# Retention's swish and row scales through Exp and Ln on ScalarE, PSUM banks from one free list, norm by tile at the start, final norm scaled ahead

## Chip, cores and metric

One Trainium2 chip, all 8 cores (two dies: cores 0 to 3 and 4 to 7). Each core computes one of the 8 batch elements; the cores exchange nothing. The metric is the time of the slowest core in microseconds (us) on the device.

Executions fall into two states: both kernels showed both, and so did 16 of the 18 kernels of the experiments. In the fast state all cores show nearly the same granted TensorE clock (0.977 to 0.982 of full speed in every fast execution of the kernel before). In the slow state the cores of one die, or of both, show a lower granted clock (0.81 to 0.98 in the runs of this study; in one execution of c15, 5663.94 us, 0.831 to 0.835 on one die and 0.993 to 0.994 on the other) and the time is up to 20% longer. This document compares fast executions alone.

Terms used below: PE is TensorE's matmul, DVE is VectorE, ACT is ScalarE, POOL is GpSimd, SP is the engine that issues most loads and stores other than weights. A *stage* is the time from the first matmul of one kind to the first matmul of the next kind.

## The reference, cut to what matters

```python
h   = modulate(rmsnorm(x, norm1_g), sh1, sc1)       # sh1, sc1, gt1...: silu(c) @ w_mod + b_mod
p   = h @ w_in                                      # q, k, v, g, u, vs, two merge gates
ret = bidirectional_retention(rope(q), rope(k), v, ...)             # 8 heads, starts from context
ret = ret * rsqrt(mean(ret * ret, -1) + EPS) * silu(g)              # row scale, swish
sg  = gelu(u) * (w_s @ layernorm(gelu(vs)) + b_s)                   # spatial mixing, 128x128
x   = x + gt1 * ((sig(gr) * (ret @ w_ret_o) + sig(gs) * (sg @ w_sg_o)) @ w_out)
h2  = modulate(rmsnorm(x, norm2_g), sh2, sc2)
x   = x + gt2 * ((silu(h2 @ w_a) * (h2 @ w_b)) @ w_ffn_out)
out = rmsnorm(x, final_norm_g)
```

Per core: 2048 positions, width 2048, 256 context positions, FFN width 5632. After the heads everything runs in two halves of 1024 positions.

## The kernel before

Program order is issue order on each engine (what that costs shows in the changed kernel's trace below, where x lands from 41.8 us on and ACT starts to norm it at 156.9); the writer of the kernel decides it by hand. SBUF tiles come from one pool of addresses, so a tile that is requested may have to wait until an earlier tile at that address is free. Weights stream through four 1 MB slots, requested by POOL.

The start. Conditions (`stA`), four x tiles and small tables are loaded; the first x tiles are normed; the decay tables are built and stored; then 16 modulation weights are used, each with its own small addition on DVE.

```python
for i, src in enumerate((c_in, cctx, n1g, n2g, lng, lnb)):
    tk = F.dma("sp", stA[16 * i:16 * (i + 1), :], src)
F.wait("pool", tk)              # no weight is requested before these landed
WS.pump()
...
load_x(xkeys[:4])
F.dma("sp", dist[:], distd); F.dma("sp", idx[:], idxd); F.dma("sp", jdx[:], jdxd)
F.dma("sp", wsf[:], sgw.rearrange("g i j -> i g j"))
...
norm_x(0, xkeys[0:4])           # ACT squares four tiles, DVE root, DVE scales four tiles
...                             # decay tables: DVE, ACT Exp, stores to tab_d
for s in range(16):
    mod_cols(s, bank(s % 4))    # 32 matmuls, then DVE adds b_mod into modp
```

The root (reciprocal square root) is 13 small DVE operations, used in every norm:

```python
def rsqrt(dst, src, n, mul):
    ... 4 operations, then three Newton steps of 3 operations on [128, n]
```

A retention head, its output block, with PSUM banks taken in turn from two fixed sets (`RA` of four, `RV` of two):

```python
def outp(b):
    ps = bank(RA.get())
    ...                                                     # 12 matmuls
    for i in range(2):
        F.act(r[:, i, :], ps[...], AF.Square, accum=ssq[:, i:i + 1])
    rsqrt(rst[:], ssq[:], 2, 1.0 / 256.0)                   # 13 DVE operations
    for i in range(2):                                      # only now is the bank read out
        F.stt("dve", r[:, i, :], ps[...], rst[:, i:i + 1], sg[:, i, :], ALU.mult, ALU.mult)

def g_unit(b, wg):
    ps = tm_pair(wg, ...)                                   # bank from RV
    F.act(sg, ps, AF.Silu)
```

Ahead of the spatial mixing the retention results, a bias table and row sums; ahead of the residual the x tiles and gate rows; at the end the final norm, all on DVE:

```python
F.dma("sp", part, ret_d[...])  # 16 loads
F.dma("sp", bsb, sgb.partition_broadcast(128))
...                            # row sums of w_s by two matmuls
rsqrt(rst[:], ssq[:], 1, 1.0 / D)
for q in range(4):
    F.stt("dve", xs, xs, rst[:], fngb[:, q * 512:(q + 1) * 512], ALU.mult, ALU.mult)
```

## Time and profile before

| | before |
|---|---|
| fast executions | 5043.67, 5044.09 us |
| profiled execution, slowest core | 5041.4 us |
| PE busy | 4655.7 us, 92% |
| matmuls at their closest spacing (estimate) | 4598 us |

The estimate counts every matmul of the trace at the spacing seen in undisturbed stretches: 216 ns for 512 columns, 109 ns for 256, 56 ns for 128, 25 ns for the two-column ones. Some 443 us are thus not matmul time, and only they can be won.

The page of the kernel before, part 1 (busy time, share of the span, number of instructions):

```profile
span 5041.4 us, 68033 instructions; the slowest of 8 cores (5014.0 to 5041.4 us)
PE 4655.7 (92%) x26671; PEld 2460.9 (49%) x26671; DVE 1438.4 (29%) x3076; ACT 803.0 (16%) x1577; POOL 483.3 (10%) x556
```

What PE waited for in the kernel before, whole span (us in total, how often, longest):

```profile
PE ps L279 <- DMA wm<-w_mod: 64.4, 10, 11.2
PE ps L279 <- DVE modp L303: 55.0, 1, 55.0
...
PE ps L279 <- DVE sTt L303: 26.5, 16, 2.2
PE ps L282 <- DVE wsb L312: 26.2, 1, 26.2
PE ps L279 <- DVE tm L307: 21.3, 7, 14.8
PE ps L279 <- DVE r L307: 21.2, 8, 3.0
...
PE ps L282 <- DVE xb L300: 18.1, 4, 15.4
```

Read: one single wait of 55 us for the addition into `modp` at the start; about 45 us in the heads (`sTt`, `r`), in pieces of 1.2 to 3.0 us; single waits in head 0 (`wsb`, `xb`) and in the mixing (`tm`).

### The profile page before, as it was taken

Reading aid. Unit: us, or ns where it says so; the run is one execution under the profiler, and the core shown is the slowest. Engines: PE = TensorE matmul, PEld = TensorE weight load, DVE = VectorE, ACT = ScalarE, POOL = GpSimd, SP = SyncE. Lnnn points to the kernel's source line nnn. Section 1 sums busy time; section 2 is a strip of 40 time slices with the busy share of each in tenths; the row PEclk is TensorE's granted clock in tenths of the full one; section 3 lists DMA queues with packets and bytes.
Section 4 is the critical chain, followed back from the end, with each engine's and each line's share of the span. In section 5 each row is a group of like instructions: output and inputs, shape, how many; then the busy total and the mean of one; then the engine's idle time right before and its main releaser. Section 6 shows DMA issues by size and latency. Waiting matters only on the chain.

```text
span 5041.4 us, 68033 instructions; the slowest of 8 cores (5014.0 to 5041.4 us)
## 1 busy us (share of the span) xinstructions
PE 4655.7 (92%) x26671; PEld 2460.9 (49%) x26671; DVE 1438.4 (29%) x3076; ACT 803.0 (16%) x1577; POOL 483.3 (10%) x556
## 2 busy tenths in 40 slices
PE   0479999999999899999999999899999999999996
PEld 0357667676664444444444444344444444444443
DVE  1244554444553311114112111434101230021015
ACT  2232222222222100013000000121000130000001
POOL 0012222122220011100000000000111000000000
PEclk9889999999999999999999999999999999999998
DMA  7743343332444434463444445554354634444443
GB/s 164 182 113 60 60 80 62 73 58 53 76 74 75 93 68 90 85 130 69 78 78 81 78 80 116 117 113 84 67 96 78 136 67 79 83 79 78 78 87 95
DMA packets 106729, 443.13 MB, mean 88 GB/s; under 512 B 10832, under 2 KB 36784, under 8 KB 63920
## 3 DMA queue, kind: packets, MB, share of 16 engines
q0 software_dynamic: 47232, 339.76, 38.2%
q1 hardware_dynamic: 59184, 99.04, 6.4%
q8 instruction: 216, 3.54, 0.3%
q14 instruction: 97, 0.79, 0.1%
HBM read 744.93 MB, written 33.57 MB: 154 GB/s over the span
## 4 chain that ended last, share of the span: by engine, by line
PE 82%; DVE 7%; DMA 5%; issue 3%; ACT 2%; SPq 1%; DVEq 0%; another core or an unknown queue 0%; ACTq 0%; POOL 0%; POOLq 0%
PE ps L279 81%; DMA xt<-x 1%; DVE rs_t L303 1%; PE ps L282 1%; SPq L260 1%; DVE rs_m L300 1%; DMA wm<-w_mod 1%; DMA x_35252<-x 1%; DVE rst L307 1%; DMA x_22924<-x 0%; DMA wk<-w_qkvg 0%; ACT r L293 0%; ACT xb L293 0%; DVE xb L300 0%; DVEq L182 0%
## 5 line engine op out<-in xcount | busy, mean ns | idle before, releaser
L279 PE MATMUL ps<-h,wfi 128*128 128x512 bf16 x5632 | 1221.5, 379 | 0.0
L279 PEld LDWEIGHTS ps<-h,wfi 128*128 128x128 bf16 x5632 | 549.9, 98 | 657.1
L279 PE MATMUL ps<-wfo,aT 128*128 128x512 bf16 x2816 | 608.4, 379 | 0.0
L279 PEld LDWEIGHTS ps<-wfo,aT 128*128 128x128 bf16 x2816 | 275.5, 98 | 332.3
L303 DVE TENSOR_TENSOR aT<-sa,ps 128x512 bf16<-128x512 f32 x176 | 121.0, 688 | 1065.0 <-PE ps L279 1057.3
L293 ACT ACTIVATE sa<-ps 128x512 f32<-128x512 f32 x176 | 104.9, 597 | 1370.9 <-PE ps L279 1370.9
L303 DVE TENSOR_TENSOR gtf<-ps,gtf 128x512 f32<-128x512 f32 x128 | 88.6, 692 | 778.7 <-PE ps L279 778.7
L279 PE MATMUL ps<-wv,h 128*128 128x256 bf16 x2304 | 264.2, 273 | 0.0
L303 DVE TENSOR_TENSOR tg<-ps,gtab 128x512 f32<-128x512 f32 x192 | 132.6, 691 | 452.7 <-PE ps L279 448.4
L279 PE MATMUL ps<-wvs,h 128*128 128x512 bf16 x1024 | 227.8, 385 | 17.0 <-DVE tg L303 17.0
L279 PE MATMUL ps<-wo,mrg 128*128 128x512 bf16 x1024 | 230.2, 383 | 11.6 <-DVE tg L303 11.6
L279 PE MATMUL ps<-h,wq 128*128 128x512 bf16 x1024 | 240.4, 391 | 0.0
L279 PEld LDWEIGHTS ps<-wv,h 128*128 128x128 bf16 x2304 | 225.5, 98 | 28.4
L279 PE MATMUL ps<-h,wu 128*128 128x512 bf16 x1024 | 235.4, 386 | 0.0
L279 PE MATMUL ps<-sgT,wgs 128*128 128x512 bf16 x1024 | 234.8, 383 | 0.0
L279 PE MATMUL ps<-wg,h 128*128 128x256 bf16 x2048 | 234.0, 273 | 0.0
L279 PE MATMUL ps<-h,wgs 128*128 128x512 bf16 x1024 | 231.5, 379 | 0.0
L279 PE MATMUL ps<-ret,wgr 128*128 128x512 bf16 x1024 | 231.5, 379 | 0.0
L279 PE MATMUL ps<-h,wgr 128*128 128x512 bf16 x1024 | 231.5, 379 | 0.0
L279 PE MATMUL ps<-h,wk 128*128 128x512 bf16 x1024 | 227.6, 379 | 0.0
L279 PEld LDWEIGHTS ps<-wg,h 128*128 128x128 bf16 x2048 | 200.1, 98 | 23.0
L293 ACT ACTIVATE gtf<-ps 128x512 f32<-128x512 f32 x128 | 76.4, 597 | 803.0 <-PE ps L279 803.0
(545 smaller groups left out, 3991.1 us busy)
## 6 DMA issues: line engine op xcount, KB each, us to landing
wfi<-w_fi POOLq DMA_DIRECT2D x88, 1024.0 KB, 8.6
wm<-w_mod POOLq DMA_DIRECT2D x48, 1024.0 KB, 12.2
wgr<-w_gret POOLq DMA_DIRECT2D x32, 1024.0 KB, 10.1
wgs<-w_gsg POOLq DMA_DIRECT2D x32, 1024.0 KB, 14.7
wfo<-w_fo POOLq DMA_DIRECT2D x32, 1024.0 KB, 8.6
xt<-x SPq DMA_DIRECT2D x16, 1024.0 KB, 14.0
wvs<-w_vs POOLq DMA_DIRECT2D x16, 1024.0 KB, 10.1
wu<-w_u POOLq DMA_DIRECT2D x16, 1024.0 KB, 9.1
```

What stands on the lines that cost most here:

```text
L260: E["e"].dma_start(out=out, in_=in_).then_inc(self.sems[k], 16)
L279: return self.op("pe", lambda e: e.matmul(out, lhsT=lhsT, rhs=rhs, start=start, stop=stop), [lhsT, rhs], [out], inc)
L282: return self.op("pe", lambda e: e.transpose(out=out, in_=in_, identity=ident), [in_, ident], [out], inc)
L293: return self.op("act", lambda e: e.activation(**kw), reads, [out] + ([accum] if accum is not None else []))
L300: return self.op(en, lambda e: e.tensor_scalar(**kw), reads, [out])
L303: return self.op(en, lambda e: e.tensor_tensor(out=out, in0=a, in1=b, op=op), [a, b], [out])
L307: return self.op(en, lambda e: e.scalar_tensor_tensor(out=out, in0=in0, scalar=scalar, in1=in1, op0=op0, op1=op1), reads, [out])
```

## The change

Its intent: keep PE from waiting at the start, in the heads, ahead of the mixing and in the final norm. It has six parts.

```diff
 # 1 start: weights requested at once; all modulation columns into one bank, one addition;
 #   the norm of the first x tiles stands behind the decay tables
-    tk = F.dma("sp", stA[16 * i:16 * (i + 1), :], src)
-F.wait("pool", tk)
+    F.dma("sp", stA[16 * i:16 * (i + 1), :], src)
+WS.limit = 18
 WS.pump()
-norm_x(0, xkeys[0:4])            # stood here, ahead of the decay tables
 ...                              # decay tables
+for key in XK[0]:
+    norm_x(key)
 for s in range(16):
-    mod_cols(s, bank(s % 4))
+    mod_mms(bank(0), 4 * s)
+mod_add(bank(0), 0, 32)
 # 2 head 0: x normed tile by tile, root as ACT Sqrt and DVE reciprocal
+F.act(xb[:], xts[key][:], AF.Square, accum=ssq[:])
+rstd_act(ssq[:], ssq[:], 1.0 / D)
+F.ts("dve", xb[:], xts[key][:], ssq[:])
 # 3 heads: root and swish from Exp and Ln; banks from one free list; later slots
-rsqrt(rst[:], ssq[:], 2, 1.0 / 256.0)
+F.act(ssq[:], ssq[:], AF.Ln, scale=1.0 / 256.0, bias=cst[:, 1:2])
+F.act(ssq[:], ssq[:], AF.Exp, scale=-0.5)
+at(slot[0] + 0.9, lambda: fin(b, pb, ps, r, ssq))     # closing product one slot later
-F.act(sg[:].rearrange("p j e -> p (j e)"), ps, AF.Silu)
+F.act(sv, ps, AF.Exp, scale=-1.0)
+F.ts("pool", sv, sv, 1e38, 1.0, ALU.min, ALU.add)
+... one slot later: F.act(sv, sv, AF.Ln); F.act(sv, sv, AF.Exp, scale=-1.0)
+... then: F.tt("dve", sv, ps, sv, ALU.mult); PB.put(pb)
-    at(n, lambda: b_step(2 * ib + 1))
-    at(n + 1, lambda: b_step(2 * ib))
+    at(n + 1, lambda: b_step(2 * ib + 1))
+    at(n + 2, lambda: b_step(2 * ib))
+PB = Banks([2, 3, 4, 5, 6, 7])                        # get() at first use, put() after last read
 # 4 mixing: layer norm on three engines; row sums stored once and loaded in each half
+F.dma("sp", rsb[:].rearrange("p g i -> p (g i)"), rsum_d, reads=["rsum"])
 # 5 residual: x tiles loaded by column block, 24 of them ahead of the next gate row
+for nb in range(1, 4):
+    for c in range(8):
+        load_x3(c, nb)
 # 6 final norm: POOL multiplies by the weight ahead, then one scale on ACT or DVE
+if g == 1 and sumsq and nb < 3:
+    F.tt("pool", xs, xs, fngb[:, nb * 512:(nb + 1) * 512], ALU.mult)
+... tail: rstd_act; DVE scales two of four pieces, ACT two
```

(Not shown: the number of semaphores for DMAs, the mixing's order, the spacing of small jobs between matmuls.)

## The prediction

> All times are for the fast state (before: 5043 us, both dies at clock 0.979).
>
> **What bounds the kernel.** TensorE: busy 92% (page, part 1). In undisturbed stretches a 128x512 matmul leaves every 216 ns (chain of waits: 3974 matmuls in 857.7 us), a 256-wide one every 109 ns, a transpose every 56 ns. So spaced, all 26,671 need about 4598 us (my estimate). Some 443 us of the 5041 us are gaps; the change can win only there. From start-to-start times of matmuls minus the spacing:
>
> 1. The first key matmul starts at 174 us. Modulation weights can stream at one per 6.3 us, but TensorE waits 55 us for one VectorE addition (waits: "PE <- DVE modp 55.0") that stands behind the first norm, which waits for x. No weight is requested from 51 to 107 us.
> 2. Head 0's keys and values, 174 to 337 us: about 85 us (single waits of 26, 16, 15 us for x tiles loaded late and normed four at a time).
> 3. Heads, eight query phases: about 8 us each, 60 in all, behind the 13-operation reciprocal root on VectorE (2.9 to 5 us) that holds PSUM banks.
> 4. Layer norm to spatial mixing: about 31 us in half 0 (15 waiting for a bias load), 15 in half 1.
> 5. x reloads for the output projection: about 13 and 11 us.
> 6. Final norm: VectorE takes 8.8 us a tile (timeline) against TensorE's 4.75 (22 x 216 ns): 22 us lost between the halves, 41 us after the last matmul starts.
>
> **What the change does.** (1) All modulation columns go to one bank, added once; norm after the decay tables: stream unbroken. Small condition loads now compete with weights. First key matmul at about 126 us: saves 48. (2) Weights held at 18, x earlier, norm by tile with root on ScalarE: saves 55. (3) VectorE loses 13 small operations per block, gains a 0.69 us product; ScalarE exchanges one 0.59 us Silu for three such passes plus two tiny ones, about 110 us in all, where it is 24% busy[...]. [...] 18 table loads instead of 9, few of them at the heads' hand-over to Gelu, none inside; each is 1283 ns (trace: 9 loads, 11.5 us[...]). Gaps 60 to 22: saves 38. (4) Three engines apply the norm, row sums stored once, mixing starts later: saves 20. (5) Column-major x reload: saves 10. (6) VectorE falls to about 3 us a tile, ScalarE to 2.5; TensorE leads: saves 17 + 30.
>
> Sum 218 us: predicted 4825 us, range 4770 to 4895. Chance of over 2% faster 0.95, within 2% 0.04, slower 0.01.
>
> **What would show it.** First key matmul near 126 us and no wait on modp; head 0's query phase starting near 235 us (337 before); about 150 us per head (154 before); ScalarE about 31% busy in heads; last 41 us shrinking to about 11; PE busy still about 4600 us, share near 96%.
>
> **What would make it wrong.** Small loads stalled behind weight loads at the start; ScalarE, in order, becoming the limit in head 0 (estimate 75 us of work in 80 us); banks held through the longer gate chain making new waits; GpSimd's added passes slowing VectorE (now a 0.17 us operation takes 2.0 us beside a GpSimd product)[...].

The 18 table loads were counted in the compiled program. The sum: 48 + 55 + 38 + 20 + 10 + 17 + 30 = 218 us.

## The result, and the profile after

| | before | after |
|---|---|---|
| fast executions | 5043.67, 5044.09 us | 4913.11, 4906.07 us |
| slow executions (not compared) | 5649.62, 5627.85 us | 5317.04, 5254.69, 5225.25 us |
| profiled, slowest core | 5041.4 us | 4911.9 us |

The changed kernel is faster: ratio 0.9734, 95% interval 0.9692 to 0.9776. Ratios here are the mean time of one kernel's fast runs over the mean of the other's fast runs of the same rounds, so they are not quite the ratio of the quoted medians. The gain is some 134 us where 218 were predicted, and both fast times lie above the predicted range.

The page of the changed kernel, part 1, and what PE waited for:

```profile
span 4911.9 us, 67001 instructions; the slowest of 8 cores (4878.7 to 4911.9 us)
PE 4632.5 (94%) x26669; PEld 2458.0 (50%) x26669; DVE 1259.7 (26%) x1965; ACT 949.8 (19%) x1900; POOL 733.5 (15%) x688
```

```profile
PE ps L279 <- DMA wm<-w_mod: 83.7, 12, 14.2
PE ps L279 <- DVE tm L307: 53.4, 6, 26.5
PE ps L282 <- DVE xb L300: 45.8, 8, 25.0
PE ps L282 <- DMA stA<-sg_ln_b: 33.1, 1, 33.1
PE ps L279 <- DVE tg L303: 9.4, 2, 5.0
...
PE ps L279 <- DMA wq<-w_qkvg: 7.6, 1, 7.6
```

The waits on `modp`, `sTt` and `r` have gone (`modp`: 55.0 to 2.0 us). But `tm` (mixing) has grown from 21.3 to 53.4, `xb` (normed x) from 18.1 to 45.8, and `stA` from 12.9 to 33.1. The change removed the waits it aimed at, and others took part of the place.

The stages, from the times of the first matmuls of each kind in the two traces (profiled core of each; the last column is the best version found below):

| stage | before | after | saved | predicted saving | best version (c12) |
|---|---|---|---|---|---|
| start, to first key matmul | 174.0 | 174.8 | −0.8 | 48 (step 1) | 149.2 |
| head 0 keys and values, to first query | 162.7 | 135.4 | 27.3 | 55 (step 2) | 138.2 |
| all heads, first query to gate projection | 1160.1 | 1097.2 | 62.9 | 38 (step 3) | 1096.4 |
| gate projection, half 0 | 128.6 | 119.7 | 8.9 | 20 (step 4), with the next | 119.6 |
| u projection and mixing, half 0 | 136.5 | 145.8 | −9.3 | | 116.8 |
| output projection, half 0 | 125.6 | 124.8 | 0.8 | 10 (step 5), both halves | 117.0 |
| gate projection, half 1, with the end of half 0 | 140.9 | 110.5 | 30.4 | 17 (step 6) | 110.5 |
| u projection and mixing, half 1 | 120.1 | 142.1 | −22.0 | in step 4 | 116.8 |
| output projection, half 1 | 123.1 | 124.0 | −0.9 | in step 5 | 117.0 |
| after the start of the last matmul | 40.8 | 10.6 | 30.2 | 30 (step 6) | 10.3 |

The remaining stages (merge, FFN) differ by under 2 us each. The table's savings sum to 127.5 of the 129.5 us between the two profiled spans. So three things need a cause: why the start gained nothing and head 0 only half, why the mixing stalls, and why the heads gained more than expected.

**The start, in the trace.** DMA issues within the first 180 us (KB each, median us from issue to landing), first before, then after:

```profile
tab_d<-tg SPq DMA_DIRECT2D x8, 512.0 KB, 2.7
...
wsf<-sg_w SPq DMA_DIRECT2D x1, 512.0 KB, 52.0
...
stA<-norm_g SPq DMA_DIRECT2D x2, 8.0 KB, 1.6
```

```profile
tab_d<-tg SPq DMA_DIRECT2D x8, 512.0 KB, 27.4
...
wsf<-sg_w SPq DMA_DIRECT2D x1, 512.0 KB, 96.7
...
stA<-norm_g SPq DMA_DIRECT2D x2, 8.0 KB, 6.4
```

The 8 KB condition loads took 1.6 us while no weights moved and 6.4 us beside the weight stream. There are six, one after the other, and their landings (four of them at 12.1, 18.8, 25.0 and 31.3 us) fall beside those of the weight tiles (13.3, 19.9, 26.0 and 31.9): one small load per 1 MB tile. Between 4.5 and 8.7 us, while the second small load was waiting, the trace has 71 packets of the weights' queue, over four for each of the 16 DMA engines, and none of SP's. Why a small load waits for about a whole tile is not shown. PE's first transpose is at 33.1 us instead of 12.9.

What the norm's engines waited for in the changed kernel between 30 and 310 us, first ACT, then DVE:

```profile
ACT tg L293 <- DVE tg L307: 49.8, 2, 45.0
ACT wdec L293 <- DMA jdx<-k_jdx: 41.3, 1, 41.3
```

```profile
DVE tg L300 <- DMA tab_d<-tg: 69.7, 2, 64.5
```

The decay tables need `jdx`, a 2 KB load that stands behind four 1 MB x tiles and two tables of 768 KB together; it takes 48.9 us and lands at 88 us. Then DVE waits up to 64.5 us for a table to be stored, because four table buffers serve eight heads and the stores move slowly behind `wsf`: the first, issued at 95.9 us, landed at 144.0, `wsf` at 136.4. ACT waits for DVE. The norm of the first x tiles, which landed at 41.8 to 66.5 us, now stands behind all that, in order, and begins at 157 us. Before, the norm stood ahead of the tables. The first instruction of the norm on ACT, before and after:

```profile
42.38 1.91 ACT L293 ACTIVATE xb<-xt 128x2048 bf16<-128x2048 f32 x1 [26.84 <-DMA xt<-x]
```

```profile
156.90 1.89 ACT L293 ACTIVATE xb<-xt 128x2048 bf16<-128x2048 f32 x1
```

The tables themselves began no later than before (88.2 us before, 88.1 after): `jdx` was late there too, at 83.5 us. What is new is the slow stores. Before, no weights were on their way between 84 and 107 us, `wsf` had landed at 84.8, and a store took 2.7 us. The unbroken weight stream, which part 1 of the change wanted, took away that quiet time.

**The mixing, in the trace.** The changed kernel around the stall (start us, length, instruction, in brackets the idle time before and what ended it), first SP's queue, then DVE and PE:

```profile
1540.32 39.09 SPq L260 DMA_DIRECT2D ret<-ret_d  x16
1579.57 0.95 SPq L260 DMA_DIRECT2D bsb<-sg_b  x1
1580.61 0.38 SPq L260 DMA_DIRECT2D rsb<-rsum_d  x1
```

```profile
1587.24 0.35 DVE L307 SCALAR_TENSOR_TENSOR addt<-rsb,fmA,bsb 128x128 f32<-128x128 f32 x1 [43.08 <-DMA rsb<-rsum_d]
...
1588.61 0.59 PE L279 MATMUL ps<-wsT,vn 128*128 128x128 bf16 x4 [26.48 <-DVE tm L307]
```

The row sums and the bias are requested behind 16 loads of retention results, and those wait for SBUF space (SP waits 44.4 us for POOL's `vn`, the layer norm's result). DVE gets the tables at 1587 us; PE has stood for 26.5 us. In half 1 the same wait is 22.2 us. The bias (`bsb`) stood last in that queue in the kernel before as well. It landed 47 and 21 us after the first u matmul of the two halves there, and 59 and 55 us after it here; the row sums, which are new in the queue, land 1.2 us behind it. Why the space comes free later in the changed kernel was not tested.

**The residual, in the trace.** The gate row of the second column block is requested behind 24 x tiles, and DVE waits for it while they load:

```profile
2172.38 0.69 DVE L303 TENSOR_TENSOR tg<-ps,gtab 128x512 f32<-128x512 f32 x1 [24.57 <-DMA gtab<-gate_d]
```

### The profile page after: what moved, and what is told of

It reads as the page before. It is cut to its first block, busy times and chain, and to the rows that moved or that the text cites. A ratio compares the mean times of both kernels' runs of the same rounds, so it can differ in the third digit from the quotient of the medians.

```text
span 4911.9 us, 67001 instructions; the slowest of 8 cores (4878.7 to 4911.9 us)
## 1 busy us (share of the span) xinstructions
PE 4632.5 (94%) x26669; PEld 2458.0 (50%) x26669; DVE 1259.7 (26%) x1965; ACT 949.8 (19%) x1900; POOL 733.5 (15%) x688
## 4 chain that ended last, share of the span: by engine, by line
PE 88%; DMA 4%; SPq 3%; ACT 2%; DVE 1%; issue 1%; another core or an unknown queue 0%; POOL 0%; DVEq 0%; ACTq 0%; POOLq 0%
PE ps L279 87%; SPq L260 3%; PE ps L282 1%; DMA jdx<-k_jdx 1%; DMA tab_d<-tg 1%; ACT xb L293 1%; DMA gtab<-gate_d 1%; DVE tg L303 0%; DMA rsb<-rsum_d 0%; DMA stA<-norm_g 0%; DMA wq<-w_qkvg 0%; ACT h L293 0%; DVE xb L300 0%; DMA stA<-c_ctx 0%
## 5 line engine op out<-in xcount | busy, mean ns | idle before, releaser
L260 POOL DMA_DIRECT2D wfi<-w_fi x88 | 46.4, 528 | 1201.2 <-PE ps L279 1164.1
```

Of the source, the lines that this page charges most:

```text
L260: E["e"].dma_start(out=out, in_=in_).then_inc(self.sems[k], 16)
```

## The experiments

Eighteen kernels ran. Each is the changed kernel with the edit shown, unless said otherwise. Ratios are to the kernel before in the same rounds; "stage" numbers are from the profiled core. All ratios are below 1, but by the verdict that asks for a clear 2% h1, h5 and t1 are "same" as the kernel before and s2 is "unclear". The time of the first key matmul differs by 4 to 11 us between the cores of one run and that of the first query by 6 to 10; the heads' stage differs by about 1 us (after, h4, h5), at most 5 (h6), apart from two slower cores of s2.

### Start: which wait holds the first key matmul

Theory A: the norm of the first x stands behind the tables in program order. Rival B: SP's ring is simply slow, and order on the engines does not matter. Later, theory C: the ring is held by one load, `wsf`, which is 1024 pieces of 512 bytes.

**s1_norm_first.** Norm of the first x tiles ahead of the tables again.

```diff
+for key in XK[0]:
+    norm_x(key)
 ab = F.tile("ab", ...)          # decay tables begin
 ...
-for key in XK[0]:
-    norm_x(key)
```

> Changed kernel, with the first norm moved back ahead of the decay tables, as before the change. Changed kernel: first key matmul at 174.8 us although the last modulation weight was used at 137 us. Theory A (the table loads and table stores, which land one per 7 us among the weight tiles, hold the in-order ScalarE and SyncE queues): norm alone helps little, because the second four tables still wait for a table store that lands at about 144 us, and ScalarE's share of the transposes and the loads of the next x stand behind them: first key matmul at 160 to 165 us, first query matmul within 12 us of the changed kernel's 310 us, total 0 to 12 us less. Theory B (the order norm-after-tables alone is the cause): first key matmul at about 143 us, first query matmul at about 280 us, total about 30 us less.

Measured: 4849.71 and 4851.83 us, ratio 0.9621 (0.9601 to 0.9642). First key matmul 161.4 us (174.8), first query 290.6 (310.1): the first is theory A's number, the second lies between the two. So the order is part of the cause. But most of the 57 us by which the ratio is better than the changed kernel's come from elsewhere: the mixing stages fell to 116.7 us in both halves. In this kernel the retention results and the two small tables were requested at 1435 to 1467 us and at 3125 to 3191, not at 1540 to 1581 and 3285 to 3320; SP's wait of 44.4 us for POOL's `vn` is gone. The likely way is that the moved tiles changed which addresses later loads get, a side effect of SBUF placement and not of the norm's order; that was not tested.

**s2_tables_early.** `dist`, `idx`, `jdx` requested ahead of the x tiles.

```diff
+F.dma("sp", dist[:], distd); F.dma("sp", idx[:], idxd); F.dma("sp", jdx[:], jdxd)
 load_x(XK[0])
-F.dma("sp", dist[:], distd); F.dma("sp", idx[:], idxd); F.dma("sp", jdx[:], jdxd)
```

> Changed kernel, with the three loads that the decay tables need (distance and index tables) issued ahead of the first x tiles; the order of norm and tables stays. Theory A (waiting table data is the cause): the exponents start at about 60 instead of 88 us, the tables are done by about 125 us, first key matmul at 143 to 150 us, next x requested at about 120 instead of 164 us, first query matmul at 270 to 285 us, total 25 to 40 us less than the changed kernel (about 4870 us). Theory B (norm order): still near 170 us, total unchanged.

Measured: 4951.19 and 4918.80 us, ratio 0.9788 (0.9744 to 0.9832); first key 174.3, first query 309.5. Theory A missed, and the numbers are those of theory B: the exponents ran at 47 instead of 88 us, and nothing came of it. The first table store, issued at 54.8 us, landed at 131.2, behind `wsf`, which landed at 122.5 (these on core 0). That gave theory C.

**s4_wsf_late.** `wsf` requested behind the second group of x tiles.

```diff
-F.dma("sp", wsf[:], sgw.rearrange("g i j -> i g j"))
 ...
 load_x(XK[2][:2])
+F.dma("sp", wsf[:], sgw.rearrange("g i j -> i g j"))
```

> Changed kernel, with one load moved: the mixing weights (1024 pieces of 512 bytes) go to the SyncE queue after the second x tiles instead of behind the first, ahead of the table stores. In the changed kernel that load took from 40 to 136 us beside the weight stream and the first table store, issued at 96, landed at 144 us. Theory C (the many small pieces of this one load hold back everything behind it in the queue, so the first four table stores land late and tables 5 to 8 wait for their buffers): the first store lands within 15 us of its issue, tables 5 to 8 follow by about 125 us, first key matmul at 143 to 152 us, first query matmul 20 to 35 us earlier than 310, total about 4880 us. Theory D (any store waits out the weight stream): first store still lands after 135 us, first key matmul over 165 us, total unchanged.

Measured: 4902.28, 4928.99, 4926.05 us, ratio 0.9757 (0.9728 to 0.9785). First key 154.3 us; the first store, issued at 95.1, landed at 108.9. So `wsf` held the ring: theory C holds nearly for the first key (it said 143 to 152). Only in part, though: the stores still land one per 8 us or so beside the weights, where in the kernel before, with no weights moving, they landed 1.5 to 2 us apart. And the first query only came at 299.3: of 20 us gained, 10 were lost again in head 0, where the build from `wsf` now waited for its late landing (PE's wait on `wsb` rose from 5.5 to 14.6 us). The total is not better than the changed kernel's: the profiled run is 10 us shorter, but the other two had cores at a clock of 0.979 to 0.982.

**s5_early_wsf.** Both edits, s2 and s4.

```diff
+F.dma("sp", dist[:], distd); F.dma("sp", idx[:], idxd); F.dma("sp", jdx[:], jdxd)
 load_x(XK[0])
 ...
 load_x(XK[2][:2])
+F.dma("sp", wsf[:], sgw.rearrange("g i j -> i g j"))
```

> Both edits: distance and index tables loaded ahead of x (alone, this changed nothing: the tables began at 47 instead of 88 us, but the first table store landed at 131 us) and the mixing weights loaded late. Theory C: stores land 10 to 15 us after issue, all tables done by about 95 us, first norm at 75 to 100 us, first key matmul 5 to 7 us after the last modulation matmul (143 to 147 us), next x requested when the 14th weight has landed (about 125 us), first query matmul at 270 to 280 us, total 30 to 40 us less than the changed kernel (about 4870 us). Theory D: as the changed kernel.

Measured: 4903.63, 4920.58, 4925.62 us, ratio 0.9752 (0.9728 to 0.9775); first key 155.5, first query 303.0. No better than s4 alone. PE waited 14.3 us for `wsb`, made of `wsf`, at 187 us. Moving the load to a later place moved the wait to its user; the user has to move as well.

### Mixing: late tables or something else

**m1_bias_first.** Both small tables requested during the gate projection.

```diff
 for nb in range(4):
+    if nb == 1:
+        F.dma("sp", bsb[...], sgb.partition_broadcast(128))
+        F.dma("sp", rsb[...], rsum_d, reads=["rsum"])
     for kh in range(2):
         w = WS.next("wvs")
 ...
-F.dma("sp", bsb[...], sgb.partition_broadcast(128))
-F.dma("sp", rsb[...], rsum_d, reads=["rsum"])
```

> Changed kernel, with the loads of the mixing bias and of the row sums moved from behind the 16 loads of retention results to the second column block of the gate projection. Theory A (the two small loads, last in the in-order queue, are what the mixing waits for): the single waits of TensorE of 26.5 and 22.2 us in the two mixing stages vanish, the stage from first u matmul to first gate matmul falls from 145.8 and 142.1 to about 119 us in both halves, total 45 to 50 us less (about 4860 us). Theory B (the weights or the three-engine norm hold the mixing): the stage stays over 135 us.

Measured: 4857.11, 4858.44, 4856.87 us, ratio 0.9635 (0.9617 to 0.9652). The mixing stages are 116.8 and 117.0 us (145.8 and 142.1), although the 16 retention loads still come as late as before, from 1538 us on. So the stall was the two small loads behind them, not the retention results, and costs some 50 us in all (by the ratios 50; the two stages together are 54 us shorter).

**m2_rsb_mm.** Row sums by matmul as in the kernel before, the bias load left in place.

```diff
-F.dma("sp", rsb[...], rsum_d, reads=["rsum"])
+for g2 in range(2):
+    b = bank(RT.get())
+    F.mm(b, onesb[:], wsT[:, g2 * 4:(g2 + 1) * 4, :]..., True, True, inc=True)
+    F.copy("dve", rsb[:, g2 * 4:(g2 + 1) * 4, :]..., b)
```

> Changed kernel, with the row sums computed on TensorE in each half as before the change instead of loaded from memory; the bias load stays last in the queue. Theory A (queue position): only one of the two small loads goes, mixing still starts when the bias has landed, about 1 us earlier; stage from first u to first gate matmul stays within 5 us of 145.8 and 142.1 us, total the same within 6 us. Theory B (reloading the row sums is the new cost): those stages fall by over 15 us.

Inconclusive: four of five executions, with the profiled one, were slow; the one fast execution took 4900.2 us. That is near the changed kernel, as it should be if the bias load alone also comes late (in the changed kernel's trace it lands 1.2 us before the row sums), but one run without a profile in the same state shows no more.

**t1_final_only.** The kernel *before* with part 6 alone, the new final norm.

```diff
+if g == 1 and sumsq and nb < 3:
+    F.tt("pool", xs, xs, fngb[:, nb * 512:(nb + 1) * 512], ALU.mult)
-rsqrt(rst[:], ssq[:], 1, 1.0 / D)
-for q in range(4):
-    F.stt("dve", xs, xs, rst[:], fngb[...], ALU.mult, ALU.mult)
+rstd_act(ssq[:], ssq[:], 1.0 / D)
+for q in (3, 0, 1, 2):
+    ...                             # 3: DVE with weight, 0: DVE scale, 1 and 2: ACT scale
```

> Kernel before, with the final norm of the change alone (three of four columns scaled ahead on GpSimd, root by Sqrt and reciprocal, the rest spread over ScalarE and VectorE). Theory A (VectorE at 8.8 us a tile against TensorE's 4.75 us was the limit of these eight tiles): the tail after the last matmul starts falls from 40.8 to about 10.6 us, the first gate-projection stage of half 1 from 140.9 to about 111 to 118 us; if the u stage of half 1 then lengthens from 120 us by 10 to 20 us, the new mixing wait of the changed kernel comes from arriving there earlier and not from the new mixing order. Total 35 to 55 us less than before. Theory B: the tail stays over 25 us.

Measured: 4997.24, 4995.79, 4993.97, 5001.53 us, ratio 0.9905 (0.9889 to 0.992): 47 us, as much as predicted for this part. After the start of the last matmul 9.9 us instead of 40.8. The gate projection of half 1 took 127.3 us instead of 140.9 (118.5 to 127.3 on the eight cores, 140.3 to 142.7 before), where 111 to 118 was expected. The mixing of half 1, now reached earlier, did not stall (119.4 us): the new stall belongs to the changed mixing, not to earlier arrival.

On DVE, the end of the kernel before, two tiles of the final norm one after the other (each begins with this reduction), and the same in the changed kernel:

```profile
4996.55 0.16 DVE L1203 TENSOR_REDUCE ssq<-ssp 128x1 f32<-128x4 f32 x1 [0.97 <-ACT junk L293]
...
5005.17 0.16 DVE L1203 TENSOR_REDUCE ssq<-ssp 128x1 f32<-128x4 f32 x1 [0.97 <-ACT junk L293]
```

```profile
4899.48 0.16 DVE L1303 TENSOR_REDUCE ssq<-ssp 128x1 f32<-128x4 f32 x1 [0.97 <-ACT junk L293]
...
4904.23 0.16 DVE L1303 TENSOR_REDUCE ssq<-ssp 128x1 f32<-128x4 f32 x1 [0.97 <-ACT junk L293]
```

8.62 us a tile became 4.75 us, which is PE's own pace (22 matmuls of 216 ns). Before, DVE was behind PE at the end of each half and PE (17.0 us in three waits for `tg` after half 0) or the last store waited for it.

**g1_gates_first.** Gate rows requested ahead of the 24 x tiles.

```diff
+gts[0, 1] = gate_tab(0, 1); gts[0, 2] = gate_tab(0, 2)
 for nb in range(1, 4):
     for c in range(8):
         load_x3(c, nb)
 ...
 for nb in range(2):
-    gts[0, nb + 1] = gate_tab(0, nb + 1)
```

> Changed kernel, with the gate rows of the second and third column block requested ahead of the 24 remaining x tiles of the output projection. In the changed kernel VectorE waited 24.6 us for such a row behind those tiles. Theory A (the row, last in the queue, stops VectorE and so the banks): the stage from first output-projection matmul to first FFN matmul falls from 124.8 and 124.0 us to 117 to 119 us in both halves, total 8 to 15 us less. Theory B (the x tiles themselves are late): stage unchanged within 2 us.

Measured: 4893.43, 4893.32, 4898.56 us, ratio 0.9703 (0.9685 to 0.972). The output projection stages fell from 124.8 and 124.0 to 117.1 and 116.8 us.

### Heads: what saved 63 us

The parts were undone one by one, alone and together. Stage from the first query to the gate projection, 1160.1 before and 1097.2 after:

| kernel | root on DVE | swish by Silu | old slots | fixed banks | stage, us |
|---|---|---|---|---|---|
| changed | | | | | 1097.2 |
| h3_silu | | x | | | 1097.4 |
| h2_fixed_banks (wrong result) | | | | x | 1098.2 |
| h4_old_slots | | | x | | 1101.7 |
| h1_dve_root | x | x | | | 1129.7 |
| h5_root_slots | x | x | x | | 1138.2 |
| h6_heads_old | x | x | x | x | 1166.6 |
| before | x | x | x | x | 1160.1 |

**h1_dve_root.**

```diff
-F.act(ssq[:], ssq[:], AF.Ln, scale=1.0 / 256.0, bias=cst[:, 1:2])
-F.act(ssq[:], ssq[:], AF.Exp, scale=-0.5)
+rsqrt(rst[:], ssq[:], 2, 1.0 / 256.0)
...
-F.act(sv, ps, AF.Exp, scale=-1.0)      # and the five steps behind it
+F.act(sv, ps, AF.Silu)
```

> Changed kernel, but in the heads Silu in one pass and the 13-operation root on VectorE, as before the change; the free list of banks and the later slots stay. The stage from first query matmul to first gate-projection matmul took 1160.1 us before and 1097.2 us after. Theory A (VectorE's root, holding banks and VectorE's order, made the gaps): the stage returns to 1140 to 1160 us, ScalarE busy falls by about 100 us, total 45 to 63 us more than the changed kernel. Theory B (the free list and the slots closed the gaps): the stage stays below 1110 us.

Measured: 4940.86, 4955.77, 4952.42 us, ratio 0.9826 (0.9806 to 0.9846); stage 1129.7. Half of the gain goes: neither theory's number.

**h2_fixed_banks.** The free list replaced by the two fixed turns; the late release stays.

```diff
-PB = Banks([2, 3, 4, 5, 6, 7])
+PB = Fixed([4, 5, 6, 7]); RV = Fixed([2, 3])     # put() does nothing
 ...
-    pb = PB.get()                                # in tm_pair, the pair products
+    pb = RV.get()
```

> Changed kernel, with the free list undone: pair products take banks 2 and 3 in turn, all else 4 to 7 in turn, as before the change; Exp/Ln stays, and with it the gate product that now holds its bank for two slots. Theory A (root off VectorE is what helped): the stage of 1097.2 us rises by less than 20 us. Theory B (free list needed): the third gate product must wait for the first one's bank, about 2 to 4 us in each of 64 blocks, the stage rises by 60 us or more.

Measured: 4920.13, 4920.10, 4910.54 us, ratio 0.9752 (0.9736 to 0.9769), stage 1098.2, with a wrong result (relative error 0.067: a bank is written again before the swish's product has read it, so this kernel does not wait where it would have to). Followed through the program, the takes and releases of banks collide at the seven hand-overs between heads alone, where the context's two pairs take banks 2 and 3 while the last two swishes still hold them; no bank of a closing product is taken early. So within the heads the 1 us stands: the list's order of banks is not itself a gain beside the fast root. What a correct kernel would wait at the hand-overs was not measured.

**h4_old_slots.** State update and closing product in their old slots.

```diff
-    at(n + 1, lambda: b_step(2 * ib + 1))
-    at(n + 2, lambda: b_step(2 * ib))
+    at(n, lambda: b_step(2 * ib + 1))
+    at(n + 1, lambda: b_step(2 * ib))
-at(slot[0] + 0.9, lambda: fin(b, pb, ps, r, ssq))
+fin(b, pb, ps, r, ssq)
```

> Changed kernel with the order of the head's small work as before the change: the two backward state steps one slot earlier, the scaling of each result right after its sums instead of one slot later. Undoing Exp/Ln alone gave back 33 of the 63 us gained in the heads. Theory A (the later slots are the other half): the stage of 1097.2 us rises by 15 to 35 us. Theory B (only VectorE's length matters): it stays below 1103 us.

Measured: 4922.15, 4925.49 us, ratio 0.9759 (0.9738 to 0.978), stage 1101.7 (1101.4 to 1102.3 on the eight cores): 4.5 us, as theory B has it.

**h5_root_slots.** h1 and h4 together.

```diff
+rsqrt(rst[:], ssq[:], 2, 1.0 / 256.0); F.act(sv, ps, AF.Silu)
+at(n, lambda: b_step(2 * ib + 1)); at(n + 1, lambda: b_step(2 * ib)); fin(b, pb, ps, r, ssq)
```

> Change: the changed kernel with the swish as one Silu, the 13-operation root on VectorE, and the backward state update one slot earlier with the closing product right behind the root, all three as before; the free list of PSUM banks stays. Measured so far on the stretch from the first query product to the first gate-projection product: before 1160.1 us, changed 1097.2, root and swish undone alone 1129.7 to 1130.2, slots undone alone 1101.7, banks undone alone 1098.2 (wrong results). Theory A: root and slots work together (a long root on VectorE in a slot that must wait for it costs more than either alone), so the stretch goes back to 1150 to 1165. Theory B: the parts add, and the stretch is 1130 to 1138; then the rest lies in something none of the three holds, the free list or the work around it.

Measured: 4947.32, 4957.05, 4964.10 us, ratio 0.9831 (0.9802 to 0.9859), stage 1138.2. The parts nearly add (32.5 + 4.5 would give 1134). Theory A falls.

**h6_heads_old.** h5 and the fixed banks; the banks are now read out soon, so the result is right.

```diff
+PB = Fixed([4, 5, 6, 7]); RV = Fixed([2, 3])     # on top of h5_root_slots
```

> Change: as h5_root_slots, and in addition the fixed banks in turn (4 for most products, 2 for the pairs) in place of the free list; since each bank is now read out soon, the order of use is the one of the kernel before and the result should be right. Theory A (root and slots together): the stretch is that of h5_root_slots within 5 us. Theory B (the free list is worth something once VectorE is slow, because a bank held late stops PE only where the next bank is fixed): h5_root_slots stays below 1140 and this one goes to 1150 to 1165. If both stay below 1140, the remainder lies outside the heads' own code, in the work that the other stages leave to them.

Measured: one fast run, 4984.74 us, correct; stage 1166.6, slightly beyond the kernel before. One run is thin, but its eight cores agree (1163.9 to 1168.8, against 1137.2 to 1138.3 in h5). So the rest lay in the free list, but only together with the slow root: with the fast root the fixed banks cost 1 us (h2, in late slots), with the slow one 28.4 (in old slots; slow root and fixed banks in late slots were not run). Of the 28.4 us, 13.9 are gaps and 14.5 slower matmuls, by the split given below. The waits of PE in this stage, first before, then h6_heads_old, then h5_root_slots:

```profile
PE ps L279 <- DVE sTt L303: 24.4, 15, 2.2
PE ps L279 <- DVE r L307: 21.2, 8, 3.0
```

```profile
PE ps L279 <- DVE sTt L303: 24.5, 15, 2.2
PE ps L279 <- DVE r L307: 21.3, 8, 2.9
```

```profile
PE ps L279 <- DVE sTt L303: 31.8, 23, 2.2
```

The waits on `r`, one a head, are waits for a bank that the closing product still holds; with fixed turns PE must take that very bank, with a free list it takes another. That they come back to within 0.1 us when the fixed banks do is the strongest evidence.

And the stages by engine, with PE's busy time and the granted clock in the column ahead of the DMA share (before, changed, h5_root_slots, h6_heads_old; same columns for all, named in the first line):

```profile
core 1: us, PE busy (x) PEld busy (x) DVE busy (x) ACT busy (x) POOL busy (x), PEclk, DMA share, GB/s
337.00:1497.00 1160.00, 1114.21 (x9178) 807.64 (x9176) 565.27 (x1355) 277.79 (x630) 251.92 (x214) 0.99 0.36 67
```

```profile
310.00:1407.00 1097.00, 1096.86 (x9172) 803.78 (x9173) 458.12 (x622) 384.90 (x874) 399.97 (x275) 1.00 0.38 71
```

```profile
308.00:1446.00 1138.00, 1105.96 (x9176) 804.53 (x9175) 564.77 (x1352) 275.98 (x627) 251.20 (x213) 0.99 0.38 69
```

```profile
311.00:1478.00 1167.00, 1120.77 (x9178) 810.35 (x9179) 565.63 (x1353) 276.37 (x627) 251.54 (x213) 0.98 0.35 67
```

The same 9,170-odd matmuls take 1114 us of busy time before and 1097 after, at a granted clock of 0.99 and 1.00. Splitting the stage of each trace into gaps over 0.5 us and the rest above the closest spacing (1094.8 us): before 49.1 us in 23 gaps and 16.2 us of slower matmuls; h1 32.6 and 2.2; h5 35.5 and 7.9; h6 49.4 and 22.4; changed 0 and 2.3. So the kernels with the longer gaps also have the slower matmuls: gaps of 1.0 to 2.0 us (h1) came with 2.2 us, of 0.9 to 2.4 (h5) with 7.9, and those with one gap of 2.5 to 3.2 us in each head (before, h6) with 16 and 22. That the gaps are the cause of the lower clock, and not something that comes with them, is not shown by a run of its own.

**h3_silu.** Only the swish goes back to one Silu; root from Ln and Exp.

```diff
-F.act(sv, ps, AF.Exp, scale=-1.0)      # and the five steps behind it
+F.act(sv, ps, AF.Silu)
+PB.put(pb)
```

> Change: only the swish goes back to one Silu on ScalarE; the row scale stays Ln and Exp on ScalarE, so ScalarE needs two tables in turn within each head. Theory A (the point of the Exp/Ln swish is that no table is loaded between): many more table loads, over 60 against 18 in the changed kernel, at about 1.28 us each, and the heads' stretch grows from 1097 to over 1115 us. Theory B (ScalarE has so much room, it is busy under a fifth of the span, that the loads are absorbed): the stretch stays within 1095 to 1105 although the loads are there; then the longer swish bought nothing.

Measured: 4912.74, 4924.69, 4910.76 us, ratio 0.9742 (0.9716 to 0.9769), stage 1097.4. Table loads, part of ACT's groups over the whole span (count, busy us and ns of one), changed kernel and h3_silu:

```profile
L293 ACT ACT_TABLE_LOAD x18 | 23.1, 1283 | 57.6 <-DVE fmA L312 33.9 <-PE ps L279 18.7 <-DVE z L303 3.3
```

```profile
L293 ACT ACT_TABLE_LOAD x128 | 164.2, 1283 | 154.3 <-PE ps L279 100.7 <-DVE fmA L312 34.4 <-DVE z L303 5.6
```

128 loads take 164 us of ACT and no time that shows in PE's stage (1097.4 against 1097.2 us). In the heads alone there is 1 load in the changed kernel, where ACT goes from Ln to Exp and back throughout, and there are 111 here, 142.4 us of ACT. The longer swish, with its 64 GpSimd passes of 2.23 us, its DVE product and its longer hold on a bank, saved nothing. From h3_silu to h1_dve_root only the root differs, and the stage goes from 1097.4 to 1129.7 us: of the 33 us of h1, then, the root is all.

### A version that beats both kernels

**c9_combined.** s5, the build from `wsf` moved to the last key unit, m1 and g1.

```diff
 if ib == 0:
-    wsT_build()
 ...
 if ib == 3:
+    wsT_build()
```

> Changed kernel with four queue edits: index tables ahead of x, mixing weights late (their transposes moved to the last key unit, so that they don't stop VectorE, as the late load did at 187 us), bias and row sums early, gate rows early. Theory: first key matmul near 150 us, first query matmul 275 to 290 us, both mixing stages near 117 us, both output-projection stages near 118 us: total 4810 to 4835 us, 1.5 to 2 per cent below the changed kernel and over 4 below the kernel before.

Measured: 4839.27 us in the profiled run, 4861.98 to 4866.13 in the five timed ones, ratio 0.9642 (0.9627 to 0.9657). First key 158.9, first query 293.2. The profiled run nearly met the expectation, the timed ones did not: in four of them some cores took about 4835 us at a granted clock of 0.993 and others about 4861 us at 0.987, in changing places; in one all eight were slow in this way. What splits them was not found.

**c10.** s1, s4 and m1, and the build from `wsf` moved; no early tables.

```diff
+for key in XK[0]: norm_x(key)                  # ahead of the decay tables
+F.dma("sp", wsf[:], ...)                       # behind load_x(XK[2][:2])
+wsT_build()                                    # at ib == 3
+F.dma("sp", bsb[...], ...); F.dma("sp", rsb[...], ...)      # at nb == 1 of the gate projection
```

> Change: a candidate that is to beat both kernels. The changed kernel with the norm of the first x tiles ahead of the decay tables, the gate table's load behind the second x tiles with its transposes at the last key unit, and both bias tables of the mixing requested during the gate projection. Theory A (the two start edits meet different waits and add up): first key product 135 to 155 us, first query product 275 to 288, mixing stretches 116.8 each, fast runs 4815 to 4840. Theory B (the start is held by the arrival of the x tiles of the second block, not by either edit): first query product 289 to 300, as in each edit alone, and fast runs 4843 to 4866, as s1_norm_first, m1_bias_first and c9_combined.

Measured: 4848.70, 4847.45, 4841.71 us, ratio 0.9604 (0.9582 to 0.9625). First key 147.6, first query 281.7: 28 us earlier than the changed kernel, where s1 gave 20 and s4 11. So two different waits stood at the start, the norm's order and `wsf`, and their gains nearly add at the first query once the user of `wsf` moves too: theory A. The time lies just above what theory A expected (and in theory B's range), because the output projection of half 1 now took 138.3 us, with DVE waiting 38.6 us for a gate row.

**c12.** c10 and g1.

```diff
+gts[0, 1] = gate_tab(0, 1); gts[0, 2] = gate_tab(0, 2)      # on top of c10
 for nb in range(1, 4):
 ...
-    gts[0, nb + 1] = gate_tab(0, nb + 1)
```

> Change: c10 with both gate rows of the first residual requested ahead of the 24 x tiles as well (the edit of g1_gates_first), because c10's own trace shows the stretch from the first output product to the first feed-forward product at 128.4 and 138.3 us with VectorE waiting 38.6 us for a gate row. Theory A (the stall is only the row behind the x tiles, and it adds to the other edits): these stretches are 116 to 119 both times, the others as in c10 within 8 us together, fast runs 4805 to 4832. Theory B (placement in SBUF moves and another load becomes late, as u of the second half did in g1_gates_first): the gain is under 12 us, fast runs 4833 to 4850.

Measured: 4820.37, 4818.90, 4818.76 us, ratio 0.9544 (0.9529 to 0.9558); the kernel before took 5045.20 to 5055.90 in the same rounds. Both output projections take 117.0 us, and every stage is within 6 us of c10's otherwise. This is the best version: 4.6% under the kernel before and some 90 us under the changed one. The three largest sums that PE still waits for in it:

```profile
PE ps L279 <- DMA wm<-w_mod: 87.0, 12, 14.2
PE ps L282 <- DMA stA<-sg_ln_b: 34.6, 1, 34.6
PE ps L282 <- DVE xb L300: 26.0, 7, 4.9
```

All three lie before the first query.

**c15.** c12 with the swish as one Silu.

```diff
-F.act(sv, ps, AF.Exp, scale=-1.0)      # and the five steps behind it
+F.act(sv, ps, AF.Silu)
```

> Change: c12 with the swish as one Silu as in h3_silu. Theory A (the table loads stay hidden under the matmuls in a kernel with less slack too): heads stretch within 3 us of c12 with 128 table loads, fast runs within 8 us of c12. Theory B (h3_silu hid them only because the changed kernel stalled elsewhere): the heads stretch is over 6 us longer than c12's.

Measured: 4818.89, 4819.61 us fast (the profiled run was slow, on die 0), ratio 0.9544 (0.9526 to 0.9561); on an undisturbed core of the profiled run the stage is 1096.5 us. So h3_silu's verdict holds where the other stalls are gone, and the simple swish is as good.

## Why the prediction was right or wrong

The direction was right, the sum was wrong: 4825 us predicted, 4906 to 4913 measured. In the table of stages, steps 1, 2, 4 and 5 missed by 49, 28, 42 and 10 us, and steps 3 and 6 gained 25 and 14 us more than predicted. By step, as the prediction numbered them:

1. *"First key matmul at about 126 us: saves 48."* Wrong: 174.8 us, nothing saved. This is the step that failed first. The wait on `modp` did vanish and the weights did stream (16th weight used at 137 us instead of 168). But the step looked at PE's wait alone and took what stood behind it, the normed x, as ready. The change had moved that norm behind the tables, and the tables behind slow stores. s1, s4 and c10 show both waits: 13 us by order, 20 by `wsf`, 27 together at the first key (medians over the eight cores: 14, 24 and 26). The prediction named the risk in one half ("small loads stalled behind weight loads") but put no time on it: the condition loads alone moved PE's first work from 12.9 to 33.1 us. With these late and the last modulation matmul at 137 us, 126 us was out of reach even with the norm ready. What an undisturbed start would give, with the condition loads landed ahead of the weights, was not run.
2. *"Saves 55"* in head 0. Half right: 27.3 us. c12 has the same stage at 138.2, so what is left there is not the mended waits. The term that failed is what remains: of 85 us above the closest spacing 30 were to stay, and 54.6 stayed (135.4 less 80.8). In the changed kernel PE waits five times for `xb`, 16.5 us in all and 4.7 at the longest; norm by tile makes ACT and DVE alternate in order (between 30 and 310 us DVE waits 18 times, 38.1 us in all, for ACT's root). A wait of 7.6 us for the weight `wq` is new: the change holds the weights at 18, so `wq`, the nineteenth, was requested at 297.7 us instead of 162.1 and landed as the first query needed it. That these are the remaining limit was read from the trace, not tested.
3. *"Gaps 60 to 22: saves 38."* The mechanism was right, the size too small: 62.9 us. The gaps went to zero, not to 22: measured by the same rule 65 us (49.1 in gaps and 16.2 of slower matmuls) became 2.3. The mis-sized term is what remains; I assumed that the `sTt` waits would partly stay. Of the gain, undoing in the order root, slots, banks gives back 32.5, 8.5 and 28.4 us (6.5 more than the gain in sum); the bank's share was seen only beside a slow root. The swish's share is 0, although the prediction costed it with care: 110 us more of ACT's time for root and swish, and it was 107.1 (384.9 less 277.8 in this stage).
4. *"Mixing starts later: saves 20."* Wrong: the gate projection gained 8.9 us in half 0, and the mixing stages lost 9.3 and 22.0. The step costed what was removed (two matmuls) and counted on the mixing, and did not ask when the two small loads at the end of a waiting queue would land: the bias, for whose wait the prediction itself has 15 us in half 0 and which the change left in its place, and the new row sums just behind it. m1 shows it: some 50 us come back when both are requested early. How much either alone costs stays open (m2).
5. *"Column-major x reload: saves 10."* Wrong: 0 in sum, since the gate row now stood behind 24 tiles. g1 shows 7 us a half once it does not.
6. *"Saves 17 + 30."* Right for the end, 30.2 us, and t1 shows 47 us for the part alone. A tile takes 2.9 us of DVE and 2.5 of ACT in the changed kernel, as predicted. Between the halves it was 30.4 us, more than 17; there the faster layer norm is in the same stage. t1, with the final norm alone, gains 13.6 us there on its profiled core, and 22 to 23 on its fastest; the rest goes to other parts, and which was not separated.

Of the signs named: the first query came at 310 us (predicted 235), a head took 146 us (predicted 150), ACT was busy 35% of the heads' stage (predicted 31%) and 69.4 us in head 0 (estimated 75), PE's share 94% (predicted 96%), the last 41 us became 10.6 (predicted 11). GpSimd's passes beside DVE, banks held through a longer chain, and ACT's load in the heads did no harm there: the changed stage has no gap over 0.5 us.

The mended kernel c12 lands at 4819 us, close to the predicted 4825, but that is partly chance: it is better in steps 3 to 6 than predicted and still worse in steps 1 and 2.

## What to carry to other kernels

When a change removes the longest wait in front of a matmul, list everything else that the matmul needs and ask, for each, when it now arrives and what stands ahead of it in its engine's order and in its DMA ring; a saving is only as large as the next arrival allows. A small table that is needed early must be requested early: here a 2 KB one behind four 1 MB tiles and 768 KB of tables took 48.9 us, and such requests, with one norm in the wrong place, cost about 90 us (the changed kernel against c12). Holding a PSUM bank was expensive here only where the next user had no other bank to take and the root was slow: the free list was worth 28 us beside the slow root and about 1 us beside the fast one. The root itself was worth some 32 us even with the list, since the matmuls also wait for data (`sTt`) that comes from the same engine.
